# Hybrid decoder layer on one core: inverting the 32x32 diagonal blocks of four token tiles in one pass of steps instead of two

## The chip, the core and the metric

The kernel runs on one core of a Trainium2 chip. Its time is that of one execution on the device, in microseconds (us). The engines are named as in the profile: PE (matrix products), DVE (vector), ACT (scalar functions), POOL (GpSimd), and SP, which here only issues DMAs. All data are float32 in memory; large products are made of three passes over a high and a low part of each operand.

## What is computed

One layer over 1024 tokens and 1024 channels. An input projection feeds two groups of heads: sliding-window attention, and a gated DeltaNet. Then come the output projection, an MLP and a gated embedding. The change lies in the DeltaNet, in the solve of the unit lower triangular 64x64 system of each chunk:

```python
k_beta = k * beta[..., None]
L = jnp.where(strict, jnp.einsum('bhncd,bhnsd->bhncs', k_beta, k) * decay, 0.0)
T = lax.linalg.triangular_solve(eye + L, jnp.broadcast_to(eye, L.shape), left_side=True, lower=True)
u = T @ v_beta;  w = T @ (k_beta * exp(g))
def step(state, inp):
    v_new = u_i - w_i @ state
    o = q_i @ state + a_i @ v_new
    state = state * d_i + k_i^T @ v_new
```

There are 4 heads and 16 chunks of 64 tokens; the state is carried from chunk to chunk.

## The kernel before, in words

Tokens go in two halves of 512, and a half has four token tiles of 128 (two chunks each). Work is emitted by generators that a small planner (`Flow`) interleaves: one stream of large projections (`projections`) as filler, and beside it the tasks `chain` (per half), `attend` and, per half, the four tasks of `pairs` (two scans, the preparations, the merges). The framework below then lists each engine's instructions by priority and data dependence with a timeline of its own; at run time every engine takes its list strictly in order.

The part around the change, for one half (lines of the kernel before):

- `norms` (L650 to L707) computes the row factors; it sends `bb` through DRAM (`BD`) and gets it back as `bS`, the factors of the rows of the 32x32 blocks (L697). It squares q and k into the buffer `rD` and puts sums into `et`.
- `pre` (L709 to L749) makes for each token tile the decay matrix (`rD` on POOL, a PE product, exp on ACT, `et` on POOL), then the products of k with k and of q with k, each times the decay on DVE (`ka`, L741). The diagonal 32x32 blocks of the first go to DRAM (`LD`, L747).
- `inverse` (L752 to L775) solves the 32x32 blocks. A token tile has 4 heads times 4 blocks, 16 blocks. It is called after the second and after the fourth tile with `g` 0 and 1, each time for 32 blocks. A block is spread over four partitions, each holding 8 of the 32 columns of the unknown (`XS`), and the block itself (`LS`) is loaded four times (L764). One product applies the row factors (L767); then 31 steps follow, each of two dependent DVE instructions (L771, L772), which take row j out of the rows below it. Their size is (31 - j) rows times min(j + 1, 8) columns. The first pass has buffers of its own, `LS` and `XS`; the second borrows `rD` and `et`. The result goes to DRAM (`XD`, L774).
- `merge` (L776 to L824) loads the blocks of one tile (`load_x`, L831), transposes them (`XT`, L792), joins the 32x32 inverses to 64x64 inverses with five groups of small PE products, and writes them over the products in `ka`.
- `prep` and `scan` (L833 to L950) use the merged tile; a scan step needs the state that the previous tile's step left (`St`, L924).
- `w_out` (from L994) is the output projection. Of its second half, three column groups do the first half of their sum early; the rest waits until all scans of the half are done.

Two facts set the order. The second half's `norms` need `rD` and `et`, which the first half's `inverse` holds to its end. And the stream on PE is the only work that PE can do while it waits for DVE; at the end of the front part of the kernel (before the MLP) that stream is the early part of `w_out`.

Of the kernel before, what the change touches and what calls it, by code (L numbers as in the profile page):

```python
# [10 lines left out]
F32 = mybir.dt.float32  # L11
F32R = mybir.dt.float32r
AF = mybir.ActivationFunctionType
ALU = mybir.AluOpType
# [4 lines left out]
P = 128  # L19
# [92 lines left out]
def hybrid_block(ctx, tc, t, out):  # L112
# [545 lines left out]
    def norms(s, q, k):  # L658

        b, free = yield from take("e")  # L660
        sq = dt_([P, 2, 4, P], "rD", bufs=1, dt=F32R).bitcast(F32).rearrange("p i h c -> p i (h c)")
        xs = [(sel[i], x[:, h, 3:], h) for i, x in enumerate((q, k)) for h in range(4)]
        for j in range(9):
            if j < 8:
                A.activation(sq[:, j % 2], xs[j][1], AF.Square)
                yield 0.99
            if j:
                m, _, h = xs[j - 1]
                T.matmul(b[h * 32:h * 32 + 32, :], m, sq[:, (j - 1) % 2],
                         start=j <= 4, stop=j > 4)  # L670
        sb = dt_([P, 4, P], "et", bufs=1).rearrange("p h c -> p (h c)")
        A.copy(sb, b)
        free()
        yield 2.38
        b, free = yield from take("e")
        for tt in range(4):
            T.transpose(b[:, tt * P:(tt + 1) * P], sb[:, tt * P:(tt + 1) * P], ident)
        for i in range(2):
            V.tensor_scalar(s["ss"][:, i].rearrange("p (t h) -> p t h", t=4),
                            b.rearrange("p (t h x) -> p x t h", t=4, h=4)[:, i], EPS, None,  # L680
                            op0=ALU.add)
        free()
        w = lambda name: dt_([P, 16], name, bufs=2)
        rk2, rk, c2d, cc, bb = w("rk2"), w("rk"), w("c2d"), w("cc"), w("bb")
        ssq, ssk = s["ss"][:, 0], s["ss"][:, 1]
        V.reciprocal(rk2, ssk)
        V.tensor_tensor(bb, s["beta"], rk2, op=ALU.mult)
        yield 3.17
        b, free = yield from take("e")
        T.transpose(b[0:16, 0:P], bb, ident)  # L690
        bT = dt_([16, P], "bT", bufs=1)
        A.copy(bT, b[0:16, 0:P])
        free()
        SY.dma_start(s["BD"], bT)
        bS = dt_([P, 2, 32], "bS")
        for x in range(4):
            SY.dma_start(bS[x * 32:x * 32 + 32], s["BD"].rearrange("(g x) (b c) -> (x b) g c", g=2, b=4))  # L697
        G.tensor_tensor(rk, ssk, mhalf, op=ALU.pow)
        sc4 = dt_([P, 4, 2, 2, 2], "sc4", bufs=2)
        v = lambda x: x.rearrange("p (t g h) -> p t g h", t=4, g=2)  # L700
        V.tensor_tensor(sc4[:, :, :, 0], v(bb), v(s["eG"]), op=ALU.mult)
        V.tensor_tensor(sc4[:, :, :, 1], v(s["beta"]), v(rk), op=ALU.mult)
        V.reciprocal(c2d, ssq)
        V.tensor_scalar(c2d, c2d, 1.0 / (128.0 * 128.0), None, op0=ALU.mult)
        G.tensor_tensor(cc, ssq, mhalf, op=ALU.pow)
        V.tensor_scalar(cc, cc, 128.0 ** -0.5, None, op0=ALU.mult)
        s.update(bb=bb, bS=bS, sc4=sc4, c2d=c2d, cc=cc)  # L707

    def pre(s, q, k, place):  # L709

        def decay(tt):
            rD = dt_([P, 2, 4, P], "rD", bufs=1, dt=F32R)
            for i, g in enumerate(("gh", "gl")):
                G.tensor_tensor(rD[:, i], bc(mle, 1, 4),
                                bc(s[g][:, tt * 4:tt * 4 + 4].bitcast(F32), 2, P), op=ALU.mult)
            return rD

        rD = decay(0)
        yield 3.3
        for tt in range(4):  # L720
            b, free = yield from take("e")
            for i in range(2):
                T.matmul(b, mgtR, rD[:, i].rearrange("p h c -> p (h c)"), start=i == 0, stop=i == 1)
            et = dt_([P, 4, P], "et", bufs=1)
            A.activation(et, b.rearrange("p (h c) -> p h c", h=4), AF.Exp)
            free()
            G.tensor_tensor(et, et, bc(mle, 1, 4), op=ALU.mult)
            if tt < 3:
                rD = decay(tt + 1)
            kap, wait = place(tt)  # L730
            for e in wait:
                yield e
            ka = dt_([P, 2, 4, P], "ka", kap, bufs=4 if kap is dn else 2)
            s["KE"][tt], s["AT"][tt] = ka[:, 0], ka[:, 1]
            sl = slice(3 + tt * P, 3 + (tt + 1) * P)
            yield 3.0
            for j, x in enumerate((k, q)):
                b, free = yield from take("e")
                for h in range(4):
                    T.matmul(b[:, h * P:(h + 1) * P], k[:, h, sl], x[:, h, sl], start=True, stop=True)  # L740
                V.tensor_tensor(ka[:, j], b.rearrange("p (h c) -> p h c", h=4), et, op=ALU.mult)  # L741
                free()
                if j == 0:
                    ld = s["LD"].rearrange("(t h b) (s c) -> t b s h c", t=4, h=4, s=32)
                    for blk in range(4):
                        r = slice(blk * 32, blk * 32 + 32)
                        SY.dma_start(ld[tt, blk], ka[r, 0, :, r])  # L747
                yield 3.02
            if tt % 2:  # L749
                inverse(s, tt // 2)  # L750

    def inverse(s, g):  # L752


        if g:
            LS = dt_([P, 2, 4, P], "rD", bufs=1, dt=F32R).bitcast(F32).rearrange("p i h c -> p (i h c)")
            XS = dt_([P, 4, P], "et", bufs=1).rearrange("p h c -> p (h c)")[:, 0:256]
        else:
            LS, XS = dt_([P, 1024], "LS", bufs=1), dt_([P, 256], "XS", bufs=1)
        y = slice(g * 32, g * 32 + 32)  # L760
        G.memset(XS, 0.0)
        for x in range(4):
            d = slice(x * 32, x * 32 + 32)
            SY.dma_start(LS[d], s["LD"][y])  # L764
            G.memset(XS[d, x * 8:256:33], 1.0)
        LS, X3 = LS.rearrange("p (s c) -> p s c", s=32), XS.rearrange("p (j i) -> p j i", j=8)
        V.tensor_tensor(LS, LS, bc(s["bS"][:, g], 1, 32), op=ALU.mult)  # L767
        for j in range(31):
            n, m = 31 - j, min(j + 1, 8)
            tp = dt_([P, 192], f"tp{g}", bufs=1)[:, 0:n * m].rearrange("y (k i) -> y k i", k=m)  # L770
            V.tensor_tensor(tp, bc(LS[:, j, j + 1:32], 1, m), bc(X3[:, 0:m, j], 2, n), op=ALU.mult)  # L771
            V.tensor_tensor(X3[:, 0:m, j + 1:32], X3[:, 0:m, j + 1:32], tp, op=ALU.subtract)  # L772
        for x in range(4):
            SY.dma_start(s["XD"][y, x * 256:x * 256 + 256], XS[x * 32:x * 32 + 32])  # L774

    def merge(s, tt):  # L776

# [308 lines left out]
    b = bank(ps["e"])  # L1086
# [349 lines left out]
```

## Time and profile before

| | |
|---|---|
| time, median of 3 runs | 1415.89 us (1413.04 to 1417.85) |
| time of the profiled execution | 1413.97 us |
| its span, first to last instruction | 1412.2 us |
| busy: PE, DVE, ACT, POOL | 97%, 50%, 35%, 35% of the span |
| mean granted clock of TensorE | 0.987 |

The span is the time from the first to the last instruction on the core; the time of the execution is 1.8 us longer. "Busy" of PE counts a pipelined matmul from start to modelled end. Where the profile says that an engine was idle, it names the engine whose instruction ended the wait. Times in the rows below are us from the start of the span.

### The profile page before, as it was taken

What the parts mean: (1) busy time and instruction counts of PE and PEld (TensorE: products, weight loads), DVE (VectorE), ACT (ScalarE), POOL (GpSimd) and SP (SyncE); (2) the same over time, 40 slices, a digit from 0 to 9 for tenths busy, and PEclk for the clock granted to TensorE, in tenths of its full rate; (3) what the DMA queues carried; (4) which work ended last, traced back from release to release, by engine and by line L of the source; (5) the groups of instructions that cost most, each with busy time, mean ns of one, the idle gap of its engine ahead of it and who ended that gap; (6) DMA issues with size and microseconds to landing.
All of it is one profiled execution on the core that took longest, in us unless ns stands there. A gap on an engine that the chain in (4) does not pass through costs nothing.

```text
span 1412.2 us, 20118 instructions
## 1 busy us (share of the span) xinstructions
PE 1369.5 (97%) x7760; PEld 1160.4 (82%) x7760; DVE 702.5 (50%) x1446; ACT 493.9 (35%) x1013; POOL 490.5 (35%) x492
## 2 busy tenths in 40 slices
PE   9989999899997999999999999999999999999997
PEld 7788778788887899888888888888888888888886
DVE  6776967998579965443121231212313223255333
ACT  7455465444343344351220312203122031344222
POOL 6673636531555343241320413204132041321222
PEclk9999999999999999999999999999999999999999
DMA  6312222223123222211210112101121011241101
GB/s 217 90 46 77 60 53 65 65 68 76 44 84 116 63 87 75 76 52 45 67 45 30 53 46 68 45 30 52 45 68 45 30 53 45 81 135 38 46 30 45
DMA packets 81200, 90.31 MB, mean 64 GB/s; under 512 B 15600, under 2 KB 63264, under 8 KB 81104
## 3 DMA queue, kind: packets, MB, share of 16 engines
q1 hardware_dynamic: 78208, 83.27, 19.9%
q10 hardware_dynamic: 2544, 4.99, 1.1%
q8 instruction: 61, 1.00, 0.3%
q0 software_dynamic: 352, 0.76, 0.2%
q14 instruction: 35, 0.29, 0.1%
HBM read 83.73 MB, written 5.26 MB: 63 GB/s over the span
## 4 chain that ended last, share of the span: by engine, by line
PE 78%; DVE 13%; DMA 3%; issue 2%; ACT 2%; POOL 1%; SPq 1%; POOLq 0%; DVEq 0%; ACTq 0%
PE bk L95 76%; DVE tp L771 2%; PE bk L99 2%; DVE cv L404 2%; DVE XS L772 1%; DMA AT<-in_xT 1%; DVE w L212 1%; POOL rsb L350 1%; DVE s L541 1%; DVE s L550 1%; DMA raw<-in_w_in 1%; DVE et L772 1%; DVE H L404 0%; ACT w L211 0%; DVE ka L741 0%
## 5 line engine op out<-in xcount | busy, mean ns | idle before, releaser
L95 PE MATMUL bk<-R,w 128*128 128x256 f32 (+1 forms) x1920 | 359.6, 334 | 4.4 <-DVE H L1014 3.0
L212 POOL TENSOR_TENSOR w<-raw,w 128x512 fp32r<-128x512 f32 x140 | 188.4, 1348 | 486.2 <-ACT w L211 382.6
L95 PE MATMUL bk<-aT,w 128*128 128x512 f32 x1536 | 349.8, 389 | 0.0
L211 ACT CAST w<-raw 128x512 fp32r<-128x512 f32 (+1 forms) x244 | 151.2, 620 | 554.5 <-PE bk L95 370.1
L95 PEld LDWEIGHTS bk<-aT,w 128*128 128x128 f32 x1536 | 288.3, 188 | 60.3
L95 PEld LDWEIGHTS bk<-R,w 128*128 128x128 f32 x1920 | 290.9, 192 | 46.9 <-issue 6.9
L212 DVE TENSOR_TENSOR w<-raw,w 128x512 fp32r<-128x512 f32 (+1 forms) x104 | 78.7, 757 | 248.4 <-ACT w L211 248.3
L95 PE MATMUL bk<-M,w 128*128 128x512 f32 x768 | 198.9, 394 | 0.0
L95 PEld LDWEIGHTS bk<-M,w 128*128 128x128 f32 x768 | 144.3, 188 | 34.5
L1295 DVE TENSOR_TENSOR H<-bk,H 128x512 f32<-128x512 f32 x96 | 64.8, 689 | 103.7 <-PE bk L95 103.7
L212 POOL TENSOR_TENSOR aT<-Z,aT 128x512 fp32r<-128x512 f32 x32 | 41.5, 1298 | 137.2 <-ACT aT L211 137.2
L95 PE MATMUL bk<-U,w 128*128 128x512 f32 (+1 forms) x384 | 76.3, 345 | 1.6 <-ACT ba L464 1.1
L95 PEld LDWEIGHTS bk<-U,w 128*128 128x128 f32 x384 | 58.4, 188 | 18.0 <-issue 7.3
L95 PE MATMUL bk<-w,R 128*128 128x256 f32 (+1 forms) x480 | 70.3, 298 | 0.1
L95 PE MATMUL bk<-w,U 128*128 128x256 f32 (+2 forms) x384 | 65.9, 326 | 3.4 <-ACT AT L470 1.6
L95 PEld LDWEIGHTS bk<-w,R 128*128 128x128 f32 x480 | 63.7, 200 | 2.5 <-issue 1.9
L95 PEld LDWEIGHTS bk<-w,U 128*128 128x128 f32 x384 | 57.2, 198 | 10.0 <-ACT AT L470 1.8
L1295 DVE TENSOR_TENSOR AT<-bk,AT 128x512 f32<-128x512 f32 x32 | 21.8, 690 | 57.0 <-PE bk L95 57.0
L547 ACT ACTIVATE s<-s,mx 128x257 f32<-128x257 f32 (+1 forms) x64 | 31.2, 490 | 50.8 <-DVE mx L545 46.4
L95 PE MATMUL bk<-R,aT 128*128 128x512 f32 (+1 forms) x204 | 47.8, 383 | 0.0
L95 PE MATMUL bk<-M,aT 128*128 128x512 f32 (+1 forms) x204 | 47.0, 378 | 0.0
L212 POOL TENSOR_TENSOR aT<-r,aT 128x512 fp32r<-128x512 f32 x32 | 45.2, 1413 | 0.2 <-ACT aT L211 0.2
(338 smaller groups left out, 1780.8 us busy)
## 6 DMA issues: line engine op xcount, KB each, us to landing
raw<-in_w_in SPq DMA_DIRECT2D x72, 256.0 KB, 2.8
raw<-in_w_up SPq DMA_DIRECT2D x64, 256.0 KB, 2.7
raw<-in_w_down SPq DMA_DIRECT2D x64, 256.0 KB, 2.9
raw<-in_w_o SPq DMA_DIRECT2D x32, 256.0 KB, 3.0
rawg<-in_w_gate SPq DMA_DIRECT2D x16, 256.0 KB, 2.9
AT<-in_xT SPq DMA_DIRECT2D x14, 256.0 KB, 3.9
out<-AT SPq DMA_DIRECT2D x7, 512.0 KB, 2.6
H<-in_xT ACTq DMA_DIRECT2D x3, 1024.0 KB, 5.1
```

The costliest lines, as they stand in the source:

```text
L95: self.tc.nc.tensor.matmul(o, lh, rh, **k)
L99: self.tc.nc.tensor.transpose(o, x, i)
L211: A.copy(hi, src)
L212: lo_eng.tensor_tensor(lo, src, hi.bitcast(F32), op=ALU.subtract)
L350: eng.tensor_tensor(acc, acc, xr, op=ALU.add)
L404: V.scalar_tensor_tensor(cv if i < 3 else x[:, 3:], x[:, i:i + HB], cw[:, j, i:i + 1], cv, op0=ALU.mult, op1=ALU.add)
L541: V.tensor_tensor_reduce(out=s[:, i, lo:256], in0=b[:, i, lo:256], in1=amask[:, lo:256], scale=1.0, scalar=NEG, op0=ALU.add, op1=ALU.max, ...
L547: A.activation(s[:, i, lo:257], s[:, i, lo:257], AF.Exp, bias=mx[:, i:i + 1], accum_out=sm[:, i:i + 1])
L550: V.tensor_tensor(s[:, :, lo:256], s[:, :, lo:256], bc(sm, 2, 256 - lo), op=ALU.mult)
L771: V.tensor_tensor(tp, bc(LS[:, j, j + 1:32], 1, m), bc(X3[:, 0:m, j], 2, n), op=ALU.mult)
L772: V.tensor_tensor(X3[:, 0:m, j + 1:32], X3[:, 0:m, j + 1:32], tp, op=ALU.subtract)
L1295: V.tensor_tensor(h, bs[m], h, op=ALU.add)
```

## The change

One pass treats the 64 blocks of all four tiles after the fourth tile: a block now lies on two partitions, each with 16 columns. The 31 steps have sizes (31 - j) times min(j + 1, 16). `LS` and `XS` are always the borrowed `rD` and `et`, and the first pass's own three buffers are gone. `LD`, `bS` and `XD` move in two DMAs of 64 partitions instead of four of 32, and each block is loaded twice instead of four times.

```diff
-        bS = dt_([P, 2, 32], "bS")
-        for x in range(4):
-            SY.dma_start(bS[x * 32:x * 32 + 32], s["BD"].rearrange("(g x) (b c) -> (x b) g c", g=2, b=4))
+        bS = dt_([P, 32], "bS")
+        for x in range(2):
+            SY.dma_start(bS[x * 64:x * 64 + 64], s["BD"].rearrange("y (b c) -> (y b) c", b=4))
...
-            if tt % 2:
-                inverse(s, tt // 2)
-
-    def inverse(s, g):
+        inverse(s)
+
+    def inverse(s):
...
-        if g:
-            LS = dt_([P, 2, 4, P], "rD", bufs=1, dt=F32R).bitcast(F32).rearrange("p i h c -> p (i h c)")
-            XS = dt_([P, 4, P], "et", bufs=1).rearrange("p h c -> p (h c)")[:, 0:256]
-        else:
-            LS, XS = dt_([P, 1024], "LS", bufs=1), dt_([P, 256], "XS", bufs=1)
-        y = slice(g * 32, g * 32 + 32)
+        rD = dt_([P, 2, 4, P], "rD", bufs=1, dt=F32R).bitcast(F32)
+        LS = rD.rearrange("p i h c -> p (i h c)")
+        XS = dt_([P, 4, P], "et", bufs=1).rearrange("p h c -> p (h c)")
         G.memset(XS, 0.0)
-        for x in range(4):
-            d = slice(x * 32, x * 32 + 32)
-            SY.dma_start(LS[d], s["LD"][y])
-            G.memset(XS[d, x * 8:256:33], 1.0)
-        LS, X3 = LS.rearrange("p (s c) -> p s c", s=32), XS.rearrange("p (j i) -> p j i", j=8)
-        V.tensor_tensor(LS, LS, bc(s["bS"][:, g], 1, 32), op=ALU.mult)
+        for x in range(2):
+            d = slice(x * 64, x * 64 + 64)
+            SY.dma_start(LS[d], s["LD"])
+            G.memset(XS[d, x * 16:512:33], 1.0)
+        LS, X3 = LS.rearrange("p (s c) -> p s c", s=32), XS.rearrange("p (j i) -> p j i", j=16)
+        V.tensor_tensor(LS, LS, bc(s["bS"], 1, 32), op=ALU.mult)
         for j in range(31):
-            n, m = 31 - j, min(j + 1, 8)
-            tp = dt_([P, 192], f"tp{g}", bufs=1)[:, 0:n * m].rearrange("y (k i) -> y k i", k=m)
+            n, m = 31 - j, min(j + 1, 16)
+            tp = dt_([P, 256], "tp", bufs=1)[:, 0:n * m].rearrange("y (k i) -> y k i", k=m)
             V.tensor_tensor(tp, bc(LS[:, j, j + 1:32], 1, m), bc(X3[:, 0:m, j], 2, n), op=ALU.mult)
             V.tensor_tensor(X3[:, 0:m, j + 1:32], X3[:, 0:m, j + 1:32], tp, op=ALU.subtract)
-        for x in range(4):
-            SY.dma_start(s["XD"][y, x * 256:x * 256 + 256], XS[x * 32:x * 32 + 32])
+        for x in range(2):
+            SY.dma_start(s["XD"][:, x * 512:x * 512 + 512], XS[x * 64:x * 64 + 64])
```

The lists of the engines move with it at three places.

DVE, second half, where before the first pass (`LS`, `XS`) ends while the second (`rD`, `et`) begins, with a scan step's instructions (L900, L932 to L939) between; first before, then now (lines behind the change are four less):

```order
L771 TENSOR_TENSOR tp_4843<-LS_4750,XS_4751 128x32
L932 TENSOR_TENSOR oss_4956<-oss_4956,c2d_2125 128x2
L771 TENSOR_TENSOR tp_5210<-rD_5198,et_5199 128x31
L772 TENSOR_TENSOR XS_4751<-XS_4751,tp_4843 128x8x4
L933 TENSOR_SCALAR oss_4956<-oss_4956 128x2
L772 TENSOR_TENSOR et_5199<-et_5199,tp_5210 128x31
L900 SCALAR_TENSOR_TENSOR vn_5122<-bk_5117,sc_4338,u_5103 128x128
L771 TENSOR_TENSOR tp_4846<-LS_4750,XS_4751 128x24
```

```order
L763 TENSOR_TENSOR rD_4970<-rD_4970,bS_4215 128x1024
L847 TENSOR_TENSOR kd_4886<-bk_4879,ex_3489 128x256
L920 SCALAR_TENSOR_TENSOR St_3384<-St_3384,ex_542,bk_4720 128x128 x2
L923 TENSOR_TENSOR oS_4654<-bk_4720,oS_4654 128x256
L767 TENSOR_TENSOR tp_4978<-rD_4970,et_4971 128x31
L768 TENSOR_TENSOR et_4971<-et_4971,tp_4978 128x31
L767 TENSOR_TENSOR tp_4981<-rD_4970,et_4971 128x60
L768 TENSOR_TENSOR et_4971<-et_4971,tp_4981 128x2x30
```

The second half's 62 steps of its first pass, which stood among the products of `pre` and the last scan steps of the first half, are gone; the one pass begins behind the last of `pre`, and its transposes for `merge` (L792, now L788) stand behind its last step, where before two of the four stood among the second pass's steps.

PE, first half, the first merge (`XT,ka`) with the stream (`R,w`) ahead of it; first before, then now:

```order
L95 MATMUL bk_3698<-R_75,w_3702 128x256 x12
L95 MATMUL bk_3698<-R_75,w_3736 128x256 x9
L95 MATMUL bk_3699<-R_75,w_3702 128x256 x5
L95 MATMUL bk_3591<-XT_3587,ka_2250 64x64 x8
L95 MATMUL bk_3602<-gg_3522,con 128x16
```

```order
L95 MATMUL bk_4062<-R_75,w_4066 128x256 x12
L95 MATMUL bk_4062<-R_75,w_4176 128x256 x10
L95 MATMUL bk_4063<-R_75,w_4066 128x256 x12
L95 MATMUL bk_4063<-R_75,w_4243 128x256
L95 MATMUL bk_3474<-XT_3470,ka_2248 64x64 x8
L95 MATMUL bk_3485<-gg_3405,con 128x16
```

Counted from the fourth tile's decay product to this merge, 317 matmuls of the stream stood there before, and 536 now; from this merge to the first merge of the second half 614 before and 627 now, beside the same 308 rows' worth of other products.

PE, second half, from the first scan step to the third tile's merge; first before, then now:

```order
L95 MATMUL bk_5570<-vn_5122,kd_5105 128x128 x2
L95 MATMUL bk_5557<-ka_4605,X_5568 64x64 x4
L95 MATMUL bk_5654<-R_75,w_5782 128x256 x4
L95 MATMUL bk_5653<-R_75,w_5860 128x256 x6
L95 MATMUL bk_5894<-R_75,w_5898 128x256 x12
L95 MATMUL bk_5895<-R_75,w_5898 128x256 x9
L95 MATMUL bk_5722<-XT_5718,ka_4868 64x64 x8
```

```order
L95 MATMUL bk_4889<-vn_4894,ka_4300 128x128 x2
L95 MATMUL bk_5488<-XT_5484,ka_4640 64x64 x5
L95 MATMUL bk_5323<-X_5334,ka_4486 64x64 x4
L95 MATMUL bk_5336<-vn_4894,kd_4877 128x128 x2
L95 MATMUL bk_5323<-ka_4486,X_5334 64x64 x4
L95 MATMUL bk_5488<-Xt_3385,Y_5497 64x64 x8
L95 MATMUL bk_5712<-XT_5708,ka_4795 64x64 x8
```

From the first merge of the second half to the scans' last product with `W` (`St,W`), 361 matmuls of the stream stood before, and 138 now, beside the same 214 other products; the third and fourth merges have moved up against the first scan step.

## Rows read from the trace of the kernel before

**Rows 1.** Windows: us, then busy (x count) of PE, PEld, DVE, ACT, POOL, clock, DMA.
```profile
242.70:333.00 90.30, 82.56 (x692) 74.41 (x690) 87.60 (x228) 38.23 (x73) 37.82 (x54) 0.98 0.25 65
407.90:490.00 82.10, 69.86 (x591) 67.11 (x590) 78.23 (x198) 26.78 (x58) 39.86 (x38) 0.92 0.29 86
...
600.00:1412.00 812.00, 803.99 (x3561) 659.09 (x3559) 244.91 (x374) 205.38 (x373) 199.37 (x162) 1.00 0.16 52
```
**Rows 2.** Waits of PE, 242.7 to 333: us in total, times, longest.
```profile
PE bk L95 <- DVE ka L741: 2.6, 1, 2.6
PE bk L99 <- DVE mx L541: 2.3, 1, 2.3
```
**Rows 3.** Waits of PE, 384 to 470.
```profile
PE bk L99 <- DVE oS L939: 7.3, 4, 2.2
PE bk L95 <- DVE H L1014: 3.0, 1, 3.0
PE bk L95 <- DVE kd L851: 1.9, 1, 1.9
```
**Rows 4.** Windows between the PE places that the lists share.
```profile
256.00:315.40 59.40, 54.96 (x409) 49.11 (x407) 57.82 (x152) 28.56 (x52) 29.09 (x47) 0.97 0.26 67
315.40:469.20 153.80, 138.98 (x1157) 126.97 (x1157) 125.03 (x301) 64.66 (x137) 68.66 (x61) 0.94 0.29 78
469.20:545.50 76.30, 76.30 (x758) 73.24 (x758) 52.75 (x148) 30.96 (x86) 32.17 (x30) 1.00 0.24 74
```
**Rows 5.** Windows of the steps alone (L771, L772): DVE busy, clock, DMA.
```profile
242.70:333.00 90.30, 39.72 (x124) 0.98 0.25 65
407.90:490.00 82.10, 51.88 (x124) 0.92 0.29 86
```
**Rows 6.** DVE timeline, second half: start, us, instruction.
```profile
458.63 1.30 DVE L772 TENSOR_TENSOR et<-et,tp 128x156 f32<-128x156 f32 x1
...
461.11 0.36 DVE L771 TENSOR_TENSOR tp<-rD,et 128x192 f32<-128x192 f32 x1
...
489.48 0.17 DVE L771 TENSOR_TENSOR tp<-rD,et 128x8 f32<-128x8 f32 x1
```
**Rows 7.** DVE timeline: the row factors of both passes of the first half, a transpose.
```profile
242.78 1.55 DVE L767 TENSOR_TENSOR LS<-LS,bS 128x1024 f32<-128x1024 f32 x1 [2.22 <-DMA LS<-LD]
275.54 1.21 DVE L767 TENSOR_TENSOR rD<-rD,bS 128x1024 f32<-128x1024 f32 x1
314.93 0.45 DVE L792 STREAM_TRANSPOSE XT<-Xt 128x256 f32<-128x256 f32 x1 [0.83 <-DMA Xt<-XD]
```
**Rows 8.** Timeline of SP's issues behind the first pass.
```profile
308.67 1.72 SPq L774 DMA_DIRECT2D XD<-XS  x4
...
311.62 3.66 SPq L831 DMA_DIRECT2D Xt<-XD  x8
```
**Rows 9.** PE timeline: merges, scan steps and a stretch of the stream.
```profile
315.43 0.68 PE L95 MATMUL bk<-XT,ka 64*64 64x64 f32 x16 [0.59 <-DVE XT L792]
...
329.31 0.28 PE L95 MATMUL bk<-ka,X 64*64 64x64 f32 x2
...
500.32 0.60 PE L95 MATMUL bk<-St,xk 128*128 128x128 f32 x4
...
521.34 0.71 PE L95 MATMUL bk<-St,W 128*128 128x128 f32 x4
...
542.78 2.90 PE L95 MATMUL bk<-R,w 128*128 128x256 f32 x23
545.51 0.61 PE L95 MATMUL bk<-St,W 128*128 128x128 f32 x4
```
**Rows 10.** DVE timeline: the state's updates in two scan steps.
```profile
511.14 0.60 DVE L924 SCALAR_TENSOR_TENSOR St<-St,ex,bk 128x128 f32<-128x128 f32 x2
...
526.28 0.60 DVE L924 SCALAR_TENSOR_TENSOR St<-St,ex,bk 128x128 f32<-128x128 f32 x2 [2.73 <-PE bk L95]
```
**Rows 11.** Window, second half, in which PE waited.
```profile
440.00:450.00 10.00, 6.86 (x38) 6.46 (x38) 9.59 (x26) 2.71 (x6) 6.35 (x10) 0.71 0.60 181
```

## Prediction, written before the changed kernel ran

> **What bounds the kernel now.** First the windows. From 600 us to the end PE is busy 804 of 812 us at full clock, in the MLP and what follows [rows 1]; nothing there belongs to the change, so the time is set by when the front part ends. In the front there are two windows in which the solve runs, one per half, from the first product with the row factors to the last step, and there DVE is the full engine: busy 87.6 of 90.3 us and 78.2 of 82.1 us [rows 1], while PE idles 7.7 and 12.2 us in them. The list of waits says for whom: in the first window PE waits for DVE's `ka` and for the attention's maximum [rows 2], around the second for the scan's `oS`, for `H` and for `kd` [rows 3]. None of these is an inversion step. They stand behind inversion steps in DVE's list. So the steps cost time by standing in the way, and the reader should see two limits: DVE in these windows, PE outside them.
>
> How much could that be worth? I cut the front at three PE places that both lists have: the fourth tile's decay product of the first half (256.0), the first merge of the first half (315.4), the first merge of the second half (469.2), and the last `St,W` (545.5) [rows 4, 9]. PE idles 4.4 us in the first stretch, 14.8 in the second, nothing in the third; the granted clock of 0.97 and 0.94 costs another 0.03 x 59.4 = 1.8 and 0.06 x 153.8 = 9.2 us [rows 4]. With the 2.6 us wait for `ka` before 256 [rows 2] that is 33 us: the ceiling of any gain here.
>
> **DVE, priced.** A step instruction took 0.17 us for 8 elements and 0.36 us for 192 [rows 6], so 0.162 us plus 0.00103 us per element. Per pass the 31 sizes sum to 3156 elements before and 4776 after, each taken twice. Two passes then cost 124 x 0.162 + 4 x 3156 x 0.00103 = 33.1 us per half; one pass of 62 instructions costs 10.0 + 9.8 = 19.9 us. The steps really took 39.7 and 51.9 us [rows 5], 20% and 57% more, because some took 1.3 us for 156 elements [rows 6] instead of 0.32. If the long ones shrink with the time, the new pass takes 23.9 and 31.2 us and DVE saves 15.8 and 20.7 us; if their number stays, 19.9 + 6.6 and 19.9 + 18.8 us, and it saves 13.2 in each. I take the first, since the long ones are spread over both passes and half of the instructions are gone. One product with the row factors of 1.2 to 1.6 us per half [rows 7] goes too. DVE saves 29 to 39 us in all, more than PE ever waited.
>
> **The small edits together.** `bS`, `LS` and `XD` go in half as many DMAs. On SP, four issues of `XD` take 1.7 us, and 6.8 us pass from the first of them to the merge [rows 8, 9]; two issues fewer there and one stream load fewer ahead of `Xt` leave about 5.4. The `memset` of the larger `XS` lies on POOL while the blocks are still under way. The freed buffers start nothing earlier.
>
> **What moves.** No merge of a half can start before the one pass ends, where two of four could before. Stretch by stretch, with 0.12 us per matmul of the stream (2.73 us for 23, from 542.78 to 545.51) [rows 9]:
>
> - *First stretch.* It gets 219 more matmuls of the stream, 26.3 us. Without the waits and the low clock, and begun 2.6 us earlier, the merge comes at 253.4 + 59.4 + 26.3 - 6.2 = 333. From DVE's side: should the pass end no earlier than the second pass did before, at 333 [rows 1], the merge comes at 333 + 5.4 = 338. I take 338, since the list keeps the last steps behind the convolutions of the stream. So the first half's merges come late, at no cost by itself: PE works on what it would have done later. The price is that the stream is used up.
> - *Second stretch.* 13 more matmuls (1.6 us) and 24.0 us to win. The tile products and the first half's scans run without steps among them, and I count their waits as gone. But the pass now stands as a whole between the last product of `pre` and the merge: 31.2 us of steps, 1.4 for the factors, 5.4 to the merge, and some updates of `H` between. Against that the list holds some 34 us of stream. PE will wait there. I give back 9 us, between none (the pass begins while scans still run) and 18. The stretch then takes 153.8 + 1.6 - 24.0 + 9 = 140 us, and the second half's first merge stands at 478, where it stood at 469.
> - *Third stretch.* It loses 223 matmuls of the stream, 26.8 us: PE's own work falls from 76.3 us [rows 4] to 49.6. But before, that stream covered a chain, which now shows. A merge takes 14.2 us (315.43 to 329.59) [rows 9]. Then, as estimates from rows: the first scan step from its new values on, 7.5; what is left of the third and fourth merges, half of a merge, 7; the second tile's step 11.4 (500.32 to 511.74) [rows 9, 10]; the third tile's step 5.5 (521.34 to 526.88) [rows 9, 10], the fourth's as much for the group that goes first; 7 us of stream that the list still has between. That is 58 us. PE then waits again, and the clock pays for it: I add 5 us. 63 us instead of 76.3.
>
> **The sum.** 338 + 140 + 63 = 541, where the place stood at 545.5: 4.5 us earlier. What follows is the same work. From the profiled execution's own 1413.97 us that gives 1409.5; since that execution is 1.9 us below the median of the three runs shown, I put the time at 1410 us. So of 33 us that DVE cost PE, some 28 are not got: 5 in the first stretch, 9 at the wait for the pass, 13 in a tail whose cover was spent earlier.
>
> **The rivals.**
>
> - *The waits stay gone.* The pass starts while the first half's scans still run, so PE hardly waits for it (2 us instead of 9), and in the tail two groups of heads overlap, so that 55 to 57 us do. Then the last `St,W` comes at 338 + 133 + 57 = 528 and the time is about 1397. For it: DVE is free by 39 us where its list was the limit. Against it: PE's list leaves only 138 matmuls of cover in the third stretch. Chance 0.22.
> - *The bare tail is slow.* It takes the place of the waits removed: when the second half's merges start, little is left for PE to do but the chain, and each of its waits lowers the clock, which slows the chain's own products. In the window in which PE waited 3.1 of 10 us the granted clock was 0.71, between the two levels of 1.2 and 2.4 GHz [rows 11]. At that clock the 49.6 us of PE work take 70, and with some waits the stretch takes 75. It decides from 67.5 us on (545.5 - 478). Then the place comes at 553 and the time is 1421. For it: before, no stretch of the front ran without cover, so no row shows the chain alone. Against it: that window had DVE busy 9.6 of 10 us [rows 11], and the tail's DVE will not be so full. Chance 0.24. The Trainium skill ("TensorE: Matmul & The Clock Gate", the section "Why this matters for your kernels") warns of just this, that gaps between bursts of matmuls put the engine back to the lower clock; by that rule alone the time would be this rival's 1421.
> - *DVE's saving is not on the path, or is smaller.* If the long instructions keep their number, the second half's pass takes 38.7 us, the merge slips by 7 us and the gain is used up: 1413.97 - 4.5 + 7 = 1416.5. The same band holds if PE's waits are only renamed, from `oS` to others in the same list. Chance 0.14.
>
> **How the numbers follow.** 0.40 is left for the forecast, 1405 to 1414 by itself: the 9 us and the 63 us are each good to some 4. What a measurement of this kernel can tell from no change is about 0.3%, 4.2 us, so faster means below 1411.6. Just over half of the forecast's case lies there: faster 0.22 + 0.22 = 0.44; the same 0.18 + 0.13 = 0.31; slower 0.24 + 0.01 = 0.25. The range goes from 1398, the first rival's price, to 1423, just beyond the second's; what it leaves out is a tail of 54 us or one of 78.
>
> **What would show it.** In the profile after: 124 step instructions instead of 248, together some 55 us instead of 91.6 [rows 5]; no wait of PE for `oS` of 2 us between the halves [rows 3]; the first half's first merge near 338, the second half's near 478, and from it to the last `St,W` about 63 us with a granted clock below 1.00, where it was 1.00 [rows 4]; PE waiting before that merge for the transpose or for the stream. I am wrong in the mechanism if PE still waits for `oS` and `ka` as before, and wrong in the price if the third stretch takes under 57 or over 68 us.

## The result, and the profile after

The changed kernel takes 1426.16 us (median of 4 runs, 1424.35 to 1427.54), the kernel before 1414.47 us beside it: a ratio of 1.0081, 95% interval 1.0061 to 1.0100. It is slower by 0.8%, where 1410 us had been forecast. The profiled execution took 1424.35 us, its span is 1422.6 us.

In what follows **D** is the second half's fourth decay product on PE (`rD,mgtR`), **M** the second half's first merge (`XT,ka`) and **S** the last `St,W`. First the PE timeline of the kernel after at the places where the prediction cut the front ([rows 4, 9] for before; start, duration, and in brackets the idle time before and what ended it):

```profile
334.41 0.68 PE L95 MATMUL bk<-XT,ka 64*64 64x64 f32 x16 [0.16 <-DVE XT L788]
420.79 0.71 PE L95 MATMUL bk<-rD,mgtR 128*128 128x512 f32 x2
492.76 0.83 PE L95 MATMUL bk<-XT,ka 64*64 64x64 f32 x16 [2.56 <-DVE XT L788]
553.36 1.22 PE L95 MATMUL bk<-St,W 128*128 128x128 f32 x4 [0.92 <-DVE Z L212]
```

The windows of the kernel after between these places, to be read against [rows 4] (length, then busy time of PE, PEld, DVE, ACT and POOL with their instructions, the granted clock, the DMA engines' share, GB/s):

```profile
251.60:334.40 82.80, 77.95 (x628) 73.15 (x626) 72.27 (x152) 39.83 (x68) 30.50 (x40) 1.00 0.30 76
334.40:492.80 158.40, 140.93 (x1172) 127.38 (x1172) 105.67 (x233) 61.44 (x135) 81.42 (x70) 0.95 0.25 71
492.80:553.40 60.60, 52.89 (x535) 48.59 (x535) 35.99 (x99) 21.47 (x69) 16.19 (x17) 0.93 0.21 65
```

The first merge stands at 334.4 (forecast 338), the third stretch takes 60.6 us (forecast 63). The second takes 158.4 us instead of 140, and that is where the forecast is lost. From S to the end of the span it is 869.2 us, 2.5 more than before. The four differences, -3.6, +18.4, -2.4 and +2.5, are the 14.9 us between 1409.5 and 1424.35.

What PE waited for in the second stretch, after (total, times, longest):

```profile
PE bk L95 <- DVE H L1010: 4.5, 3, 3.7
PE bk L99 <- DVE oS L935: 3.5, 3, 1.6
PE bk L95 <- DVE XT L788: 2.7, 2, 2.6
PE bk L95 <- DVE St L920: 1.5, 1, 1.5
```

The wait for `oS` is smaller than before [rows 3], but others stand in its place. Idle time is 158.4 - 140.9 = 17.5 us and the low clock costs 0.05 x 158.4 = 7.9: 25.4 us, where before it was 24.0. Nothing was won in this stretch. It splits at D. Up to D, from the start of the span, before and then after:

```profile
0.00:420.23 420.23, 396.62 (x2798) 341.35 (x2799) 331.53 (x759) 217.78 (x472) 218.37 (x264) 0.98 0.29 79
0.00:420.79 420.79, 400.71 (x2900) 346.89 (x2901) 313.85 (x686) 222.59 (x476) 225.50 (x260) 0.99 0.29 78
```

PE has done 102 matmuls more in the same time, some 12 us of work by the 0.12 us per matmul of the prediction: so far the change does win. The windows D to M and M to S of the kernel before:

```profile
420.23:469.24 49.01, 38.77 (x284) 37.31 (x283) 47.48 (x125) 18.04 (x42) 23.72 (x24) 0.90 0.34 98
469.24:545.51 76.27, 76.27 (x758) 73.25 (x758) 52.75 (x148) 30.92 (x86) 32.18 (x30) 1.00 0.24 74
```

and of the kernel after:

```profile
420.79:492.76 71.97, 58.12 (x418) 55.07 (x416) 54.61 (x118) 22.52 (x53) 30.46 (x27) 0.88 0.29 85
492.76:553.36 60.60, 52.90 (x534) 48.59 (x534) 36.03 (x99) 21.43 (x69) 16.19 (x17) 0.93 0.21 65
```

D stands at the same time in both. From there to the merge it is 23 us more, and the third stretch gives back only 15.7. From D to S, PE has 90 matmuls less to do (952 against 1042), and it takes 7.3 us longer: the 12 us are lost there and more. What lies between D and M is seen on DVE's timeline:

```profile
425.67 0.68 DVE L741 TENSOR_TENSOR ka<-bk,et 128x512 f32<-128x512 f32 x1
...
437.76 1.23 DVE L763 TENSOR_TENSOR rD<-rD,bS 128x1024 f32<-128x1024 f32 x1 [6.07 <-DMA rD<-LD]
...
440.08 0.18 DVE L767 TENSOR_TENSOR tp<-rD,et 128x31 f32<-128x31 f32 x1
...
484.93 1.21 DVE L768 TENSOR_TENSOR et<-et,tp 128x16 f32<-128x16 f32 x1
492.26 0.45 DVE L788 STREAM_TRANSPOSE XT<-Xt 128x256 f32<-128x256 f32 x1 [6.12 <-DMA Xt<-XD]
```

and on SP's queue of DMA issues:

```profile
426.38 1.73 SPq L747 DMA_DIRECT2D LD<-ka  x4
429.47 1.09 SPq L760 DMA_DIRECT2D rD<-LD  x2
...
486.17 1.11 SPq L770 DMA_DIRECT2D XD<-et  x2
489.12 3.66 SPq L827 DMA_DIRECT2D Xt<-XD  x8
```

The fourth tile's product of k with k, from which the blocks are taken, ends at 426.35. They go out with four stores, and the load is issued at 429.47; 11.4 us pass from the end of the product until the product with the factors starts, 2.3 with the factors and what follows them, 46.1 from the first step to the last, and 6.1 to the transpose: 65.9 us, one behind the other. Of the 46.1 us the steps take 33.0:

```profile
251.60:334.40 82.80, 23.83 (x62) 1.00 0.30 76
334.40:492.80 158.40, 32.97 (x62) 0.95 0.25 71
```

(the step instructions alone, per stretch: length, DVE busy, clock, DMA.) The rest is other work of DVE among them, 9.5 us that no step overlaps, and 3.6 us in which DVE did nothing. The groups of DVE's instructions from 427 to 493 us show whose (busy time, mean ns of one, idle time before them):

```profile
L767 DVE TENSOR_TENSOR tp<-rD,et 128x112 f32<-128x112 f32 (+27 forms) x31 | 17.1, 551 | 0.7
L768 DVE TENSOR_TENSOR et<-et,tp 128x112 f32<-128x112 f32 (+27 forms) x31 | 15.9, 513 | 0.9
L1010 DVE TENSOR_TENSOR H<-bk,H 128x512 f32<-128x512 f32 x7 | 4.7, 678 | 0.0
L1198 DVE TENSOR_TENSOR rsb<-rsb,sq 128x512 f32<-128x512 f32 x5 | 4.5, 906 | 0.0
```

Before, the same trip through DRAM was hidden: the second pass's product with the factors, in the window 420 to 470 us of the kernel before, waited for nothing (last figure), since the first pass was still being stepped through:

```profile
L767 DVE TENSOR_TENSOR rD<-rD,bS 128x1024 f32<-128x1024 f32 x1 | 1.2, 1214 | 0.0
```

### The profile page after: what moved, and what is told of

The parts are those of the page before. It is cut to its first block, busy times and chain, and to the rows that moved or that the text cites. A ratio compares the mean times of both kernels' runs of the same rounds, so it can differ in the third digit from the quotient of the medians.

```text
span 1422.6 us, 19952 instructions
## 1 busy us (share of the span) xinstructions
PE 1371.8 (96%) x7760; PEld 1160.9 (82%) x7760; DVE 676.7 (48%) x1320; ACT 493.3 (35%) x1012; POOL 486.8 (34%) x478
## 4 chain that ended last, share of the span: by engine, by line
PE 77%; DVE 13%; DMA 4%; issue 2%; ACT 2%; POOL 1%; SPq 1%; POOLq 0%; DVEq 0%; ACTq 0%
PE bk L95 75%; PE bk L99 2%; DVE tp L767 2%; DVE et L768 2%; DVE cv L404 1%; DMA raw<-in_w_in 1%; DVE w L212 1%; DMA H<-in_w_in 1%; DMA Xt<-XD 1%; DMA rD<-LD 1%; SPq L827 1%; DVE s L550 1%; POOL rsb L350 1%; DVE s L541 0%; DVE oS L935 0%
## 5 line engine op out<-in xcount | busy, mean ns | idle before, releaser
L212 POOL TENSOR_TENSOR w<-raw,w 128x512 fp32r<-128x512 f32 x140 | 188.4, 1348 | 518.8 <-ACT w L211 396.3
L95 PE MATMUL bk<-R,w 128*128 128x256 f32 (+1 forms) x1920 | 352.8, 333 | 10.8 <-DVE H L1010 4.5
L212 DVE TENSOR_TENSOR w<-raw,w 128x512 fp32r<-128x512 f32 (+1 forms) x104 | 81.8, 787 | 247.7 <-ACT w L211 247.3
L212 POOL TENSOR_TENSOR aT<-Z,aT 128x512 fp32r<-128x512 f32 x32 | 41.7, 1303 | 134.5 <-ACT aT L211 134.5
L95 PE MATMUL bk<-U,w 128*128 128x512 f32 (+1 forms) x384 | 76.3, 345 | 1.2 <-ACT ba L464 0.7
L212 POOL TENSOR_TENSOR aT<-r,aT 128x512 fp32r<-128x512 f32 x32 | 45.3, 1418 | 0.2 <-ACT aT L211 0.2
L547 ACT ACTIVATE s<-s,mx 128x257 f32<-128x257 f32 (+1 forms) x64 | 31.2, 490 | 38.8 <-DVE mx L545 34.9
```

The source lines that it names most:

```text
L95: self.tc.nc.tensor.matmul(o, lh, rh, **k)
L212: lo_eng.tensor_tensor(lo, src, hi.bitcast(F32), op=ALU.subtract)
L547: A.activation(s[:, i, lo:257], s[:, i, lo:257], AF.Exp, bias=mx[:, i:i + 1], accum_out=sm[:, i:i + 1])
```

## The experiments

The theory (A): in the second half the single pass is a chain of load, steps and store behind the last tile product, 72 us from D to M whatever PE has to do, and half of its length is not the steps' own work. Rivals: (B) the first half's pass uses the stream up early, and the end of the front has no cover in either half; (C) the lists were only reshuffled. The table has all runs; ratio is to the kernel before on the same chip.

| run | time, us | ratio (95%) | D to M | M to S |
|---|---|---|---|---|
| before | 1413.2 to 1415.2 | 1 | 49.0 | 76.3 |
| after | 1426.16 | 1.0081 (1.0061 to 1.0100) | 72.0 | 60.6 |
| one pass in first half alone | 1418.74 | 1.0031 (1.0019 to 1.0043) | 60.7 | 67.4 |
| one pass in second half alone | 1420.92 | 1.0050 (1.0038 to 1.0063) | 71.5 | 59.8 |
| after, own buffer | 1418.89 | 1.0026 (1.0014 to 1.0039) | 66.4 | 60.7 |
| after, `H` loads moved | 1424.79 | 1.0071 (1.0059 to 1.0083) | 72.2 | 62.1 |
| after, half of second pass | 1406.38 | 0.9937 (0.9924 to 0.9949) | 47.2 | 67.5 |
| after, low parts on ScalarE | 1408.53 | 0.9961 (0.9948 to 0.9974) | 59.3 | 61.2 |
| own buffer, early factors | 1413.69 | 0.9988 (0.9980 to 0.9997) | 60.6 | 62.4 |
| before, early factors | 1419.77 | 1.0030 (1.0020 to 1.0040) | 55.9 | 77.1 |
| own buffer, early, low parts on DVE | 1410.50 | 0.9983 (0.9973 to 0.9993) | 69.4 | 55.1 |
| after, low parts on DVE | 1418.97 | 1.0043 (1.0030 to 1.0055) | 75.6 | 53.1 |
| before, low parts on DVE | 1410.08 | 0.9980 (0.9971 to 0.9988) | 52.3 | 70.4 |
| after, half of first pass | 1417.77 | 1.0026 (1.0016 to 1.0036) | 71.8 | 67.1 |

### One half at a time

Both kernels hold the old and the new solve; `bS` has the layout that its half needs.

```diff
+            if tt % 2 and not s["one"]:
+                inverse2(s, tt // 2)
-        inverse(s)
+        if s["one"]:
+            inverse1(s)
```

One pass in the first half (`hb == 0`):

> One pass in the first half, two passes in the second. Theory A (the second half's single pass is the loss: its load, steps and store all lie behind the last tile product, and PE has too little left to cover them): the first merge of the first half stays near 334 us as after the change, the first merge of the second half comes near 475 instead of 493, and the time is 1406 to 1416, at or below the kernel before. Rival B (the loss is the stream that the first half uses up early, which leaves the end of the front part without cover in either case): the time stays at 1421 to 1428. Rival C (the lists were only reshuffled, and no part of the change has a cost of its own): no order between this kernel and its mirror image; both within 3 us of 1420.

One pass in the second half (`hb == 1`):

> Two passes in the first half, one in the second: the mirror image. Theory A: the first half's first merge is back at 315 us, the second half's first merge still comes late, 480 to 490, and the time is 1420 to 1430, as slow as the whole change or slower, since the 7 us won in the first half are gone. Rival B (stream used up by the first half): 1411 to 1418, as before. Rival C: within 3 us of 1420, as its mirror image.

Measured: 1.0031 and 1.0050, which add up to the 1.0081 of the whole change. Each half costs something of its own; neither A nor B holds alone. The times also lie within C's band, but the traces don't. With one pass in the second half alone D to M is 71.5 us as after the change; with one pass in the first half alone it is 60.7, against 49.0 before. The windows D to M and M to S of this last kernel:

```profile
421.25:481.96 60.71, 46.59 (x346) 43.22 (x344) 56.41 (x173) 19.74 (x49) 25.99 (x24) 0.94 0.34 98
481.96:549.39 67.43, 60.87 (x607) 56.49 (x606) 39.53 (x107) 24.30 (x74) 23.70 (x23) 0.95 0.21 67
```

The merge comes at 482 and not at 475 as A expected; the third stretch has 151 matmuls less than before, some 18 us, and is shorter by only 8.8. That is rival B's mechanism at work in the first half's share: the stream was spent early and the chain behind M shows.

### The parts of the chain

A buffer of its own for the blocks, each tile's blocks loaded as soon as they are stored:

```diff
                         SY.dma_start(ld[tt, blk], ka[r, 0, :, r])
+                    y = tt * 16
+                    for x in range(2):
+                        SY.dma_start(LS[x * 64 + y:x * 64 + y + 16], s["LD"][y:y + 16])
...
-            SY.dma_start(LS[d], s["LD"])
```

> The changed kernel with a buffer of its own for the blocks (the 4 KB that the first of two passes had), so that each tile's blocks are loaded as soon as they are stored and only the fourth tile's trip lies ahead of the pass; eight small loads instead of two. Theory A with the trip through DRAM as a part of the block: DVE's wait for the load (6.1 us) falls to 2 to 4, the second half's first merge comes 3 to 4 us earlier, the time is 1421 to 1424. If the trip is only latency and the buffer's freeing plays no part: no change, 1425 to 1428.

Measured: D to M is 5.6 us shorter, the time 1.0026 instead of 1.0081, more than expected. The chain of waits shows where in the changed kernel the load stood in it and where in this one (start, us, what; "issue" is time for which the profile names no wait); first after:

```profile
429.97 7.66 DMA rD<-LD
```

then with the own buffer, where the fourth tile's two loads of 64 KB are all that is left of it:

```profile
429.89 3.40 DMA LS<-LD
433.29 3.08 issue
436.37 1.22 DVE LS L764
```

The first of the two loads landed at 433.29, the second, issued at 430.25, only at 436.29, 6.0 us later; DVE started 0.08 us after that, so the 3.08 us are the wait for it (last figure, of the loads of the blocks from 424 to 440 us):

```profile
DMA to landing us min/median/max: 2.1/2.8/6.0
```

The trip from the end of the product of k with k is 9.7 us here and 11.4 after the change: 1.7 of the 5.6 us. Another 3.2 lie between the first step and the last (42.9 against 46.1). So the trip is part of what the change costs, but this buffer mended little of it. Whether two other loads lengthen it was the next question:

```diff
+        if not hb:
+            load_h()
...
         if hb:
+            load_h()
             yield pairs_done[1]
```

> The changed kernel with the two loads of the residual for the second half's output projection (1 MB each, issued at 429 to 430 us, just as the blocks are loaded) put behind the early parts of that projection. If these 2 MB hold up the load of the blocks: the trip from issue to landing falls from 8 us to 4 or 5, DVE's wait from 6.1 to 2 or 3, and the time to 1421 to 1424. If the trip is mere latency: trip and time as in the changed kernel, 1425 to 1428, or slower should the late load hold up the end of the projection.

Measured: no difference from the changed kernel (the intervals overlap), DVE's wait 6.3 us. The edit missed its target: the two loads are still there (issued at 429.82 and 430.32), although the first of them is one that the edit meant; the other belongs to the first half's output projection. The lists of all engines are, instruction for instruction, those of the changed kernel, so this run is a second measurement of it and tells nothing of the loads. After the change the two are issued 0.04 and 0.09 us after `St,H` products of the first half's last scan, which read `H`, so they can't simply go earlier.

What they do to the trip can be read from other traces, though no run moved them alone. The loads of the blocks, two of 256 KB (median from issue to landing): after the change, where the `H` loads are issued beside them; with the low parts on ScalarE (further down), where these come 0.6 us behind them:

```profile
rD<-LD SPq DMA_DIRECT2D x2, 256.0 KB, 6.5
```

```profile
rD<-LD SPq DMA_DIRECT2D x2, 256.0 KB, 3.8
```

The second of the two loads, on which the pass waits, took 7.4 to 8.0 us in the four traces of the first kind (after, `H` loads moved, half of second pass, low parts on DVE after the change), and 4.0 to 4.3 us in the three in which the `H` loads come 0.6 us behind it or over 6 us ahead (low parts on ScalarE, one pass in second half alone, half of first pass). So some 3.5 us of the trip go with these two loads.

Now the steps themselves, cut in the second half:

```diff
-        for j in range(31):
+        for j in range(16 if s is s01[1] else 31):
```

> The changed kernel, with the second half's pass cut after 16 of 31 steps (the blocks of that half are then not fully inverted; nothing else is left out). The 30 instructions that go are worth 9 us by their sizes and about 16 with the long ones among them. Theory A (between the second half's last tile product and its first merge there is a chain on DVE, and its length sets when the merge comes): from the last tile's decay product to the first merge 72 us become 56 to 62, and the time falls to 1410 to 1417. Rival B (PE's own list and the waits for other things stand there; the pass is hidden): the stretch stays above 68 and the time above 1422.

Measured: 1406.38 us, 20 less than the changed kernel, beyond the lower end of A's range. Its windows D to M and M to S:

```profile
419.81:467.03 47.22, 36.43 (x284) 33.32 (x282) 35.67 (x83) 15.85 (x42) 18.30 (x18) 1.00 0.35 100
467.03:534.51 67.48, 65.42 (x669) 62.00 (x669) 39.25 (x103) 28.07 (x80) 28.80 (x26) 1.00 0.24 74
```

30 instructions less make D to M 25 us shorter. The end of the pass sets the merge; rival "the pass is hidden" is out. The steps left out are 16.9 of the 25 us (33.0 less the 16.1 that the other 32 took); other work of DVE among them fell from 12.2 to 6.3 us, and DVE's idle time there from 3.6 to 0.5. The list moved with the edit: D to M holds 284 matmuls instead of 418, and so fewer updates of `H` lie among the steps. The run tells what a shorter pass is worth together with the list that follows from it, not the steps by themselves.

Next, why steps are long. Three steps of the pass after the change, on DVE, and GpSimd's instructions at the same time:

```profile
469.22 1.42 DVE L767 TENSOR_TENSOR tp<-rD,et 128x176 f32<-128x176 f32 x1
470.68 1.44 DVE L768 TENSOR_TENSOR et<-et,tp 128x176 f32<-128x176 f32 x1
472.15 0.33 DVE L767 TENSOR_TENSOR tp<-rD,et 128x160 f32<-128x160 f32 x1
```

```profile
469.16 1.29 POOL L212 TENSOR_TENSOR w<-raw,w 128x512 fp32r<-128x512 f32 x1 [2.42 <-ACT w L211]
470.62 1.29 POOL L212 TENSOR_TENSOR w<-raw,w 128x512 fp32r<-128x512 f32 x1 [0.18 <-ACT w L211]
```

The two steps that start while L212 runs end 0.2 us after it (470.64 against 470.45, 472.12 against 471.91); the third, beside none, takes 0.33 us. To see whether that is cause or chance, GpSimd's part of the output projection's weights was given to ScalarE, as a second copy of the high part (the kernel leaves the true low part out):

```diff
+        if lo_eng is A:
+            A.copy(w[:, 0], raw)
+            A.copy(w[:, 1], raw)
...
-                    w = wunit2(t["w_o"], kt // 2, g * 256, (G, G)[hb])
+                    w = wunit2(t["w_o"], kt // 2, g * 256, (A, A)[hb])
```

> The changed kernel, with the low parts of the output projection's weights made by ScalarE, as a second copy of the high part, instead of by GpSimd (the low parts are then wrong; the work on PE is the same). 13 of the 62 step instructions of the second half's pass took 0.8 us or more, and each of them lay beside a GpSimd instruction of L212, while none of the 49 short ones lay inside one. If GpSimd's instruction holds up DVE's: at most 4 of 62 are long, the steps take 20 to 24 us instead of 33, the first merge comes 7 to 13 us earlier and the time is 1413 to 1420. If the coincidence has another cause (the two start together because they wait for the same thing): 10 or more long ones, and no change beyond 3 us.

Measured: 1408.53 us, and the steps between D and M fall to 23.3 us:

```profile
416.58:475.90 59.32, 23.30 (x62) 0.88 0.32 98
```

Four of 62 are long, and these four lie beside what L212 still does on GpSimd (`R` instead of `w`), for example the two of 1.45 and 1.39 us at 444.01 and 445.50 beside two of GpSimd's from 443.92 to 446.61. Cause, not chance; 10 us of the pass are GpSimd's. The time fell by more than the 6 to 13 us expected: from the first step to the last it is 34.1 us instead of 46.1, but the trip is shorter too, 7.8 us instead of 11.4, by the later `H` loads. M is no longer set by the pass here: its transpose ends at 473.45, and M comes at 475.90 behind the stream in PE's list.

### The first half's share, and what can be mended

In the second half the first tile product comes at 393.5 after the change, 380.0 before. To see whether the scalar factors (`scalars`) are what delays it, they were moved into the first part of the program, on top of the own buffer and on the kernel before:

```diff
-        yield kv_done[hb]
-        if hb:
-            yield inv_done[0]
-        yield from scalars(s, hb)
+        if not hb:
+            yield kv_done[hb]
+            yield from scalars(s, hb)
...
+    def scalars1():
+        yield kv_done[1]
+        yield from scalars(s01[1], 1)
+        sc_done.done = True
```

> The kernel with a buffer of its own for the blocks and loads tile by tile (run above, 1418.9), and besides the second half's scalar factors are computed in the first part of the program instead of after the first half's pass. In the one-pass kernels the second half's first tile product comes 14 us later than before the change (393.5 against 380). If the place of those factors in the lists is what delays it: the first tile product comes 5 to 14 us earlier and the time is 1408 to 1416. If the delay has another cause (the squares of q and k stand behind the first half's merges in PE's list): no change, 1417 to 1421.

> The kernel before the change, with the second half's scalar factors computed early as in the run beside it. It tells whether that edit has a worth of its own without the change. If the second half of the front is set by a chain in two passes too: 1405 to 1413. If before the change PE's work is the limit there (it is busy 76.3 of 76.3 us in the third stretch): 1412 to 1418.

Measured: 1413.69 us, but the first tile product stays at 396.1 (396.5 without the edit). So the factors do not delay it; the time fell because the second to fourth tile products follow faster and D to M is 60.6 us. In this stretch the trip is 5.8 us instead of 9.7: the fourth tile's loads are issued 0.7 us and more ahead of the `H` loads and land after 2.1. On the kernel before the same edit loses 0.3%, outside both ranges, with D to M 6.9 us longer. It is no gain of its own. If it is only the lists' order that loses there, as is likely but not shown, then order alone is worth some 0.3%, and the shares of the two halves, 0.3 and 0.5%, may hold a part of that kind; no run separates it.

Then the low parts on DVE, which pays for them itself (`(G, G)[hb]` becomes `(V, V)[hb]`), on three kernels:

> The version with own buffer, loads tile by tile and early scalar factors (1413.7), with the low parts of all the output projection's weights made by DVE (0.79 us each on DVE) instead of by GpSimd (1.3 us each, in which DVE stands still). With 12 to 16 of them beside the second half's pass, DVE pays 9 to 13 us for them and gets 13 to 17 back from long steps. If that balance is what counts: the steps take 20 to 25 us, and the time is 1407 to 1413. If the low parts on DVE push the pass back in DVE's list by what they cost, and PE's list (now 335 matmuls of the stream ahead of the second half's first merge, 245 without the edit) uses up the rest of the cover: 1414 to 1420.

> The changed kernel with the same edit alone. The wrong-valued run that put the low parts on ScalarE gained 17 us; here DVE pays for them itself. If the long steps are what the change's second half suffers from: steps 20 to 25 us instead of 33 and the time 1416 to 1424. If the payment eats it: 1425 to 1430.

> The kernel before the change with the same edit: 17 of the 87 steps of its second half between 408 and 470 us were long, about 17 us. If that matters before the change as after it: 1405 to 1411. If before the change the steps are off the path (PE busy 76.3 of 76.3 us in the third stretch) and DVE only gets fuller: 1413 to 1420.

Measured: 0.9983, 1.0043 and 0.9980; the steps take 24.9 us in the first and 27.3 in the second. The edit is worth 0.4% on the changed kernel and 0.2% on the kernel before. After the change D to M is even longer with it, 75.6 us, since DVE now makes the low parts there; the gain lies in M to S. So two versions beat both kernels by a hair, and they don't differ from each other: with these costs mended, one pass is as good as two, and no better.

Last, the first half's pass cut:

```diff
-        for j in range(31):
+        for j in range(16 if s is s01[0] else 31):
```

> The changed kernel with the first half's pass cut after 16 of 31 steps (that half's blocks are then not fully inverted; nothing else is left out). The second half's pass is whole. The program's lists then put the first merge of the first half back where it stood before the change (325 matmuls of the stream ahead of it; 317 before, 536 with the change). If the first half's single pass costs by ending late, so that the second half's norms and tile products start late (14 us) and the stream is spent ahead of them: the first half's merge at 316 to 320, the second half's first tile product at 380 to 384, and the time 1417 to 1421, as in the run with one pass in the second half alone (1420.9). If only the second half's pass counts in the changed kernel: 1424 to 1428.

Measured: 1417.77 us, in the range of the first case, though the places came 6 and 10 us earlier than expected:

```profile
309.60 0.68 PE L95 MATMUL bk<-XT,ka 64*64 64x64 f32 x16 [2.19 <-DVE XT L788]
370.04 0.63 PE L95 MATMUL bk<-rD,mgtR 128*128 128x512 f32 x2
483.63 0.68 PE L95 MATMUL bk<-XT,ka 64*64 64x64 f32 x16 [0.49 <-DVE XT L788]
```

The second half's first tile product follows the first half's first merge by 60.4 us here, by 59.1 after the change, 64.6 before, 58.6 and 64.6 with one pass in one half alone. So a late first merge delays the second half, as the first half's share of the loss has it. (The profiled execution took 1421.55 us, 3.8 above the median; its S is only 2.6 us earlier than after the change.) And D to M is 71.8 us again, with 503 matmuls in it instead of 418: the second half's pass takes its time whatever PE has to do. Why the tile products follow the merge (PE's list, in which the sums of `norms` stand behind it, is the nearest reason) was not tried by itself.

## Why the prediction was wrong

- **Steps: right.** 31.2 and 23.9 us were forecast, 32.97 and 23.83 measured, by the price per element and instruction and the share of long ones. Why some were long was not known; that their share stayed was an assumption that held.
- **First stretch: right in sum.** 338 forecast, 334.4 measured; it wins some 7 us against the stream that it takes over, and that stream is missing later, as said. The two terms from DVE's side were off in opposite ways: the pass ended at 326.5 and not at 333, and from there to the merge it took 7.9 us and not 5.4.
- **Third stretch: right.** 63 forecast, 60.6 measured, at a clock of 0.93. The chain does show when its cover is gone. One trace fixes it no better than to a few us: in five traces with 534 to 543 matmuls it took 59.8 to 67.1 us, at clocks from 0.98 to 0.85.
- **Second stretch: the step that failed.** It read "31.2 us of steps, 1.4 for the factors, 5.4 to the merge, and some updates of `H` between", 38 us against 34 us of stream, and from that gave back 9 us. The chain measured 65.9, and 66.4 with the transpose, to the merge. The trip of the blocks through DRAM ahead of the pass, 11.4 us, was not in the sum: in the trace of before it waits for nothing, because another pass covers it, and the rows that were read there [rows 8] were those of the result's trip alone. The "updates of `H`" were named and not priced; with the sums of `rsb` and the last scan steps they and the waits are 13 us between the first step and the last. The way from the last step to the merge took 6.6 us and not 5.4. So 9 us should have been some 25, and the 24 us to win were all given back. (The sum itself adds up to 1409.5 us; with the 1.9 us that it names it would be 1411.4 and not 1410, which changes nothing here.)
- **Waits that "go".** `oS` and `ka` went down as forecast, but PE idled 17.5 us where it had idled 14.8: the single pass holds up `H`, `St` and `XT` instead. A third rival had this as "renamed", at 0.14.
- **The rival that came nearest in time came there for another reason.** "The bare tail is slow", 1421 us, had a third stretch of 75 us at a clock of 0.71; it took 60.6 at 0.93. Only the very end looks like it, after the change:

```profile
540.00:550.00 10.00, 7.80 (x55) 6.99 (x53) 6.18 (x16) 3.96 (x14) 3.89 (x4) 0.89 0.16 53
545.00:550.00 5.00, 2.80 (x12) 2.07 (x10) 3.16 (x9) 1.18 (x5) 1.74 (x2) 0.78 0.33 107
550.00:560.00 10.00, 7.68 (x31) 6.60 (x32) 4.45 (x16) 3.44 (x14) 0.78 (x2) 0.50 0.01 2
```

  From 550 to 560 us PE is busy three quarters of the time and the clock is 0.50, the lower of its two levels of 1.2 and 2.4 GHz; in the 5 us before, PE was busy for 2.80. The rule of the Trainium skill ("TensorE: Matmul & The Clock Gate", "Why this matters for your kernels") that was weighed for this rival, that idle gaps between bursts of matmuls bring the lower clock back, is borne out in direction for these 10 us only: the waits there were several and short, none over 1.2 us, and no whole stretch ran at 0.71. The 2.5 us lost behind S lie beside it.

## What to carry to other kernels

Two passes with half the width, of which the first runs while the next tiles are still made, can beat one pass that does the same with less work: what counts is how much stands behind the last input, and there a merged pass puts its load, all of its steps and its store in a row. When pricing such a block, walk from the last instruction that feeds it to the first that needs it and put in every DMA trip, what else is being loaded at that moment, and all that the engine's list has in between; a trip that the old trace shows with no wait may only be covered by what the change takes away.

## What the runs showed of the hardware

A DVE product or difference of two operands in SBUF that started during one of GpSimd's stood still until that had ended: 13 of the 62 steps of the second half's pass took 0.8 us or more, each beside an L212 on GpSimd; none of the others lay inside one; with most of the L212 gone 4 were left, beside the rest. In the first half's pass three short steps did lie inside an L212; there GpSimd's instruction was the longer, up to 1.84 us instead of 1.29. The updates of `H`, which read one operand from PSUM, kept their 0.68 us. The Trainium skill ("SBUF — State Buffer", "Who interferes with whom") says that such a DVE instruction contends with a GpSimd instruction that reads SBUF, and that the later one blocks until the first is done; the runs agree. The price was 10 us of one pass; the kernel without most of it was 17 us faster, a part of which is the shorter trip.

A load of 256 KB issued beside two loads of 1 MB on another queue took 7.4 to 8.0 us to land, and 4.0 to 4.3 us where these came later or were some us ahead (seven traces).
